# First feed-forward's begun blocks: fetches and stores in another order, TensorE's order written out, 1/rms applied by two engines

## The chip, the core and the metric

The kernel runs on one core of one Trainium2 chip. A core has TensorE (PE in the profile, its weight loads PEld), VectorE (DVE), ScalarE (ACT), GpSimd (POOL) and SyncE (SP, which here only issues transfers). The engines run side by side, each one in the order in which its instructions stand, and wait for each other through semaphores. SBUF is the working memory, PSUM (8 banks of 128x512 float32) takes TensorE's products. The metric is the time of one execution on the device, in microseconds (us).

## What is computed

An encoder layer on two sequences of 512 tokens of width 1024 (`x_prompt`, `x_sample`), in float32. The case is about its first step, a SwiGLU feed-forward behind an RMS norm:

```python
def rms_norm(x, g):
    xf = x.astype(jnp.float32)
    y = xf * lax.rsqrt(jnp.mean(xf * xf, axis=-1, keepdims=True) + EPS)
    return (y * g.astype(jnp.float32)).astype(x.dtype)

def swiglu(x, w_gate, w_up, w_down):
    return (jax.nn.silu(x @ w_gate) * (x @ w_up)) @ w_down
...
    x = x + 0.5 * swiglu(rms_norm(x, ffn1_norm), ffn1_w_gate, ffn1_w_up, ffn1_w_down)
```

Attention, an mLSTM memory, a second feed-forward and a last norm follow; the change doesn't touch them.

## The kernel before

**Products.** The gate and up products of both sequences are made together, column block by column block (22 blocks j of 128 columns, `NF`). The contraction of 1024 and the two operands (gate, up; prompt, sample) are each halved, and the 2x2 products are made in seven instead of eight (a Strassen scheme): B11, B21, B22, T1 to T4 name the seven pairs of left and right sums. Each float32 value is split in a high part (ScalarE copies it, rounded) and a low part (VectorE subtracts the copy), and a half product (`product`, L285) is 12 matmuls of 128x512: 4 steps of the contraction by high x high, high x low, low x high.

**Begun blocks.** The gate product of the prompt needs only B11 and B21, so the kernel begins 12 blocks (`AHEAD[0]`) with these two half products while the operands of the others are still being prepared, stores what comes out in `kept` (DRAM), and takes it back when the block is completed. Of these twelve, blocks 0 to 5 (`RAW`) are multiplied before 1/rms of the prompt is known, with x times the gain (`split_x`), and scaled by 1/rms afterwards; blocks 6 to 11 use the normed x. The parts, with their lines:

- `left(j)` (L1261): the weight block is fetched (`fetch_next`, L1206, 512 KB, four buffers `wr`), its high half copied by ScalarE (L248), its low half subtracted by VectorE (L249), into one of four tiles `w8`. `raws` holds blocks whose fetch was issued earlier.
- `lower(j)` (L1268): the half product B11 into a PSUM bank. Blocks 0, 1, 2, 7, 8, 10 and 11 use the three banks `mm`, blocks 3, 6 and 9 the one bank `pso` (PO), 4 and 5 the two `pss`. `evac(j)` (L1276): ScalarE copies the bank out (v1), and from block 6 on SP stores it. `upper(j)` (L1282): B21 on top, in the same bank, behind `evac(j)`.
- `end(j)` (L1285): blocks below 6 are scaled by 1/rms, the bank (L1290) and v1 (L1291), by VectorE; ScalarE's Silu; stores of v1 and of the gate value (L1293, L1297). Blocks from 6 on need only Silu. Their v1 and gate values take turns in two rows (`rings.k`), so a copy waits for the store of the row's last user.
- `squares(s, b)` (L1246): ScalarE's sums of squares of 128 rows of sequence s; `root(s)` (L1250): 1/rms by eleven small VectorE instructions; `spread(s, r)` (L1253): four transposes by TensorE into a bank and one ScalarE copy give 1/rms along the free axis. `normed(ks)` (L1256): x of the prompt times gain and 1/rms. The sample's x is multiplied by its gain by ScalarE (L1368) and by 1/rms by GpSimd (L1391), eight tiles of 128x512.
- `hi_all`, `lo_all`, `both` (L1302 to L1311) split the right operands. Behind the begun blocks stand the sums of T1 (L1407) and T2 (L1413), and the first full block (`gu_left_b`, L263; `gu_rest`, L307), whose first product is T2 (in the trace, the first `pss` product behind 100 us).

**What sets the order.** A scheduler places instructions by priority and by its own estimate of time. `pin` (`tc.keep_in_program_order`) holds an instruction behind those of its own engine that were pinned before it. Before the change, ScalarE's, VectorE's and GpSimd's work in this stretch and the fetches are pinned; TensorE's half products and transposes and the stores to `kept` are not.

**Queues.** All these transfers are issued by SP, in order: one that waits for its data holds those behind it. [...]

Of the kernel before, what the change touches and what calls it, by code (L numbers as in the profile page):

```python
# [26 lines left out]
def encoder(ctx, tc, I, outs):  # L27
# [154 lines left out]
                                    op=ALU.add))  # L182
        return c

    def bcast_psum(r):

        pr = PT()
        for b in range(4):
            nc.tensor.transpose(pr[:, b * P:(b + 1) * P], r[:, b:b + 1].to_broadcast([P, P]), ident)
        return pr  # L190

    def fetch_w(view):
# [89 lines left out]
            left.update({T1: wd, T3: part(wc, 0), T4: part(wc, 1)})  # L282
        return more

    def product(p, w, xt, first):  # L285
        wh, wl = w
        for k in range(HK_):
            for i, (a, b) in enumerate(((wh, 0), (wh, 1), (wl, 0))):
                nc.tensor.matmul(p, a[:, k, :], xt[:, b, k, :], start=(first and k == 0 and i == 0),  # L289
                                 stop=(k == HK_ - 1 and i == 2), skip_group_check=True)  # L290

    def gu_first(W, xc, rows, between=None):

# [10 lines left out]
            nc.scalar.activation(g0, X, AF.Silu)  # L304
        return v1, g0

    def gu_rest(W, xc, got, ring, mid):  # L307

        Y, Z = PS(), PT()
        second = lambda: product(Y, W[T2_], xc[T2_], True)  # L310
# [67 lines left out]
    class Up:  # L378
# [33 lines left out]
        def rest(self, raw, at=None, hook=None, left=None):  # L412
            ring, ORDER = self.ring, self.order

            def resume(j, pin=lambda i: i):
                got = ring.v(), ring.h()
                for t, d in zip(got, self.kept.pop(j)):
                    pin(nc.sync.dma_start(t[:, 0], d))
                return got

            if left is None:
                left = {}
                gu_left_b(*raw, ring, left)()
            raw = self.fetch(ORDER[1])
            got = resume(ORDER[0], tc.keep_in_program_order)
            for i, j in enumerate(ORDER):
                W, more = left, None
                nxt = ORDER[i + 1] if i + 1 < NF else None
                if nxt is not None:
                    left = {} if nxt in self.kept else gu_left_a(raw[0])  # L430
                    more = gu_left_b(*raw, ring, left)
                    raw = self.fetch(ORDER[i + 2]) if i + 2 < NF else None
                then = []
                h = gu_rest(W, self.xc, got, ring, lambda: then.append(resume(nxt)) if nxt in self.kept else None)
# [764 lines left out]

    in_rows = A([P, 4, D], F32, "xrows")  # L1200

    def load_rows(s):
        for b in range(4):
            pin(nc.sync.dma_start(in_rows[:, b, :], xins[s][b * P:(b + 1) * P, :]))

    def fetch_next(j):  # L1206
# [14 lines left out]
    load_x(0, 6, 8)  # L1221
    load_half(1, 1)
    raws = {2: fetch_next(2)}
    load_rows(0)
    raws[3] = fetch_next(3)

    rings = up.ring
    held_rows = [t[:, i] for t in rings.x.rows[:3] for i in range(2)]
# [22 lines left out]
        return rstd_cols(row_sq[s], 4, D, pin)  # L1251

    def spread(s, r):  # L1253
        pin(nc.scalar.activation(R[s], bcast_psum(r), AF.Copy))

    def normed(ks):  # L1256
        for k in ks:
# [10 lines left out]
    def lower(j):  # L1268
        if j < RAW:
            bank, row = (MM, MM, MM, PO, PS, PS)[j], held_rows[j]  # L1270
        else:
            bank, row = MM if j % 3 else PO, rings.k()
        begun[j] = bank(), row
        product(begun[j][0], W[j][B11], (xr[0] if j < RAW else xc[B11]), True)

    def evac(j):  # L1276
        X, v1 = begun[j]
        pin(nc.scalar.activation(v1, X, AF.Copy))
        if j >= RAW:
            nc.sync.dma_start(kept[j][0], v1)  # L1280

    def upper(j):  # L1282
        product(begun[j][0], W[j][B21], (xr[1] if j < RAW else xc[B21]), False)

    def end(j):  # L1285
        X, v1 = begun.pop(j)
        up.kept[j] = kept[j]
        if j < RAW:
            g0 = gate_rows()
            pin(V_.tensor_tensor(g0, X, R[0], op=ALU.mult))  # L1290
            pin(V_.tensor_tensor(v1, v1, R[0], op=ALU.mult))  # L1291
            pin(nc.scalar.activation(g0, g0, AF.Silu))
            nc.sync.dma_start(kept[j][0], v1)  # L1293
        else:
            g0 = rings.k()
            pin(nc.scalar.activation(g0, X, AF.Silu))
        nc.sync.dma_start(kept[j][1], g0)  # L1297

    def halves(s):
        return [x_t[s][:, i * HK_:(i + 1) * HK_, :] for i in range(2)]  # L1300
# [10 lines left out]
        lo_all(m, src)  # L1311

    (x0l, x0u), (x1l, x1u) = halves(0), halves(1)

    first_left(0, 0)
    for k in range(HK_):
# [13 lines left out]
    upper(1)  # L1330
    left(2)
    squares(0, 0)
    left(3)
    squares(0, 1)
    squares(0, 2)
    lower(2)
    lower(3)
    left(4)
    evac(2)
    squares(0, 3)  # L1340
    evac(3)
    r = root(0)
    raws[5] = fetch_next(5)
    raws[6] = fetch_next(6)
    for k in range(0, KD, 2):
        load_x(1, k, k + 2)
    raws[7] = fetch_next(7)
    load_rows(1)
    left(5)
    spread(0, r)  # L1350
    upper(2)
    upper(3)
    normed(range(4))
    end(0)
    hi_all(B11, x0l)
    lower(4)
    normed(range(4, 8))
    lower(5)
    evac(4)
    hi_all(B21, x0u)  # L1360
    upper(4)
    lo_all(B11, x0l)
    lo_all(B21, x0u)
    evac(5)
    upper(5)
    for k in range(KD):
        x = x_t[1][:, k, :]
        pin(nc.scalar.activation(x, x, AF.Copy, scale=g1[:, k:k + 1]))  # L1368
        if k == 1:
            left(6)  # L1370
        if k == 3:
            end(1)
            squares(1, 0)
        if k == 5:
            left(7)
            squares(1, 1)
    end(2)
    squares(1, 2)
    lower(6)
    squares(1, 3)  # L1380
    lower(7)
    evac(6)
    end(3)
    upper(6)
    r = root(1)
    spread(1, r)
    evac(7)
    upper(7)
    for k in range(KD):
        x = x_t[1][:, k, :]  # L1390
        pin(G_.tensor_tensor(x, x, R[1], op=ALU.mult))  # L1391
    end(4)
    end(6)
    left(8)
    end(5)
    end(7)
    left(9)
    lower(8)
    lower(9)
    evac(8)  # L1400
    left(10)
    upper(8)
    evac(9)
    upper(9)
    t2s, t4s = rings.h.rows[1:], rings.o.rows[1:]
    two = lambda t, i: t[:, 2 * i:2 * i + 2, :]
    pin(V_.tensor_tensor(x0l, x1l, x0l, op=ALU.subtract))  # L1407
    left(11)
    end(8)
    end(9)  # L1410
    raw0 = up.fetch(up.order[0])
    for i in range(2):
        pin(V_.tensor_tensor(t2s[i], two(x1u, i), two(x0l, i), op=ALU.subtract))  # L1413
    xc[T2_] = xc_tile()
    for i in range(2):
        k2 = slice(2 * i, 2 * i + 2)
        pin(nc.scalar.activation(xc[T2_][:, 0, k2, :], t2s[i], AF.Copy))
        pin(V_.tensor_tensor(xc[T2_][:, 1, k2, :], t2s[i], f(xc[T2_][:, 0, k2, :]), op=ALU.subtract))
    lower(10)
    lower(11)  # L1420
    evac(10)
    hi_all(T1, x0l)
    evac(11)
    upper(10)
    upper(11)
    W0 = {}
    more = gu_left_b(*raw0, rings, W0, pin)
# [6 lines left out]
    for i in range(2):  # L1434
        pin(V_.tensor_tensor(t4s[i], two(x0u, i), t2s[i], op=ALU.subtract))
    both(B22, x1u)
    xc[T4] = xc_tile()
    for i in range(2):
        put(xc[T4], slice(2 * i, 2 * i + 2), t4s[i])

    def sums_of(k, turned, gain):
        x0l, x0u, x1l, x1u = [up.ring.x() for _ in range(4)]
# [232 lines left out]
```

## Time and profile before

| | us |
|---|---|
| median of 3 runs (2121.76 to 2124.85) | 2123.9 |
| the profiled execution | 2121.88 |
| its span in the profile | 2120.1 |
| TensorE busy with matmuls in the span | 2069.4 (98%) |
| VectorE, ScalarE, GpSimd busy | 1559.2, 944.6, 110.0 |
| mean granted clock of TensorE in the span | 0.993 of full speed |

The profile is one execution. Its page gives each engine's busy time, the span in 40 slices, the transfers, the chain of waits that ended last, and the costliest groups of instructions. Other views list the instructions in order of time ("start us, us, engine line op out<-in xcount", with, in brackets, the idle time of that engine just before and what ended it), who waited for whom, and each engine's busy time in chosen windows, with the clock that TensorE was granted. A row with x12 merges twelve instructions of one kind that follow each other. In the chain that ended last TensorE has 86%, VectorE 6%, ScalarE 4%. In the first 200 us TensorE is busy 176.2 us.

### The profile page before, as it was taken

The numbers are of one execution on the slowest core, as the hardware profiler recorded it, in microseconds if no ns is written. First come the engines' busy times: TensorE is split into PE (matmuls) and PEld (weight loads), VectorE is DVE, ScalarE is ACT, GpSimd is POOL, SyncE is SP. The second block draws the span as 40 slices with busy tenths as digits, with TensorE's granted clock in tenths as the row PEclk, the third lists the DMA queues.
The fourth block names the chain that finished last, engine by engine and source line by source line (L and its number), as shares of the span: only waits on it lengthen the run. The fifth ranks groups of instructions, "written<-read, shape, count | busy, mean of one in ns | idle before, by whom it ended". The sixth has DMA issues, their size and how long they took to land.

```text
span 2120.1 us, 26131 instructions
## 1 busy us (share of the span) xinstructions
PE 2069.4 (98%) x9416; PEld 1687.4 (80%) x9416; DVE 1559.2 (74%) x2550; ACT 944.6 (45%) x1575; POOL 110.0 (5%) x113
## 2 busy tenths in 40 slices
PE   8799999999999999999999999999999999999997
PEld 6578888888888777878887777788788888888886
DVE  6498787886796796574649865754887877776687
ACT  6344443442225466463436555544534434343224
POOL 0200000001000110100101101010000000000002
PEclk9899999999999999999999999999999999999999
DMA  7445655699764221223342222344546444369753
GB/s 273 170 153 179 229 178 179 225 354 370 274 220 161 80 70 61 89 90 115 123 141 75 75 90 80 120 148 174 171 151 231 175 173 175 143 247 393 282 209 139
DMA packets 141777, 370.15 MB, mean 175 GB/s; under 512 B 13936, under 2 KB 13952, under 8 KB 140624
## 3 DMA queue, kind: packets, MB, share of 16 engines
q1 hardware_dynamic: 140656, 366.44, 48.7%
q0 software_dynamic: 560, 1.26, 0.3%
q8 instruction: 74, 1.21, 0.2%
q10 hardware_dynamic: 432, 0.79, 0.1%
q14 instruction: 55, 0.45, 0.1%
HBM read 263.02 MB, written 105.41 MB: 174 GB/s over the span
## 4 chain that ended last, share of the span: by engine, by line
PE 86%; DVE 6%; ACT 4%; DMA 2%; issue 1%; SPq 0%; POOL 0%; ACTq 0%; DVEq 0%; POOLq 0%
PE pss L289 17%; PE mm L698 14%; PE pst L289 11%; PE mm L289 8%; PE mm L542 8%; PE pst L542 4%; PE pss L542 4%; PE mm L682 4%; PE mm L1127 3%; PE pso L542 3%; PE pso L954 2%; PE pso L682 1%; DMA wr<-in_ffn_w_gate_dram 1%; PE pss L926 1%; PE pso L1083 1%
## 5 line engine op out<-in xcount | busy, mean ns | idle before, releaser
L289 PE MATMUL pss<-xc,w 128*128 128x512 f32 x1632 | 389.8, 389 | 0.2 <-DVE w L249 0.2
L289 PEld LDWEIGHTS pss<-xc,w 128*128 128x128 f32 x1632 | 306.2, 188 | 64.8 <-DVE w L249 0.6
L698 PE MATMUL mm<-xh,w 128*128 128x512 f32 x896 | 292.6, 396 | 0.9 <-DVE w L207 0.9
L248 ACT ACTIVATE w<-wr 128x1024 fp32r<-128x1024 f32 (+1 forms) x134 | 139.9, 1046 | 259.5 <-PE pst L289 132.6
L289 PE MATMUL mm<-xc,w 128*128 128x512 f32 x936 | 231.8, 397 | 13.9 <-ACT w L248 7.9
L249 DVE TENSOR_TENSOR w<-wr,w 128x1024 fp32r<-128x1024 f32 (+1 forms) x134 | 161.8, 1209 | 110.7 <-ACT w L248 110.5
L289 PEld LDWEIGHTS mm<-xc,w 128*128 128x128 f32 x936 | 176.9, 191 | 57.6 <-ACT w L248 8.8
L207 DVE TENSOR_TENSOR w<-wr,w 128x1024 fp32r<-128x1024 f32 (+1 forms) x112 | 135.3, 1208 | 116.5 <-ACT w L206 115.5
L698 PEld LDWEIGHTS mm<-xh,w 128*128 128x128 f32 x896 | 167.1, 188 | 33.5 <-DVE w L207 1.3
L542 PE MATMUL mm<-w,rt 128*128 128x512 f32 x792 | 185.3, 389 | 0.0
L698 PE MATMUL mm<-xl,w 128*128 128x512 f32 x448 | 176.9, 395 | 0.0
L542 PEld LDWEIGHTS mm<-w,rt 128*128 128x128 f32 x792 | 148.5, 188 | 30.7
L206 ACT ACTIVATE w<-wr 128x1024 fp32r<-128x1024 f32 (+1 forms) x112 | 114.6, 1030 | 109.8 <-PE pso L1127 35.0
L289 PE MATMUL pst<-xc,f 128*128 128x512 f32 x528 | 127.8, 389 | 0.5 <-ACT f L244 0.5
L289 PE MATMUL pst<-xc,w 128*128 128x512 f32 x528 | 127.5, 389 | 0.0
L289 PEld LDWEIGHTS pst<-xc,f 128*128 128x128 f32 x528 | 99.0, 188 | 21.6 <-ACT f L244 1.1
L289 PEld LDWEIGHTS pst<-xc,w 128*128 128x128 f32 x528 | 99.0, 188 | 20.9 <-DVE xc L1307 0.2
L602 ACT ACTIVATE w<-t 128x512 fp32r<-128x512 f32 x82 | 51.6, 632 | 122.4 <-PE pst L542 63.6
L602 ACT ACTIVATE w<-wr 128x512 fp32r<-128x512 f32 x72 | 44.5, 631 | 127.9 <-PE pso L542 68.0
L698 PEld LDWEIGHTS mm<-xl,w 128*128 128x128 f32 x448 | 84.3, 188 | 16.0
L542 PE MATMUL pss<-w,rt 128*128 128x512 f32 x396 | 94.4, 389 | 0.6 <-ACT w L602 0.6
L542 PE MATMUL pst<-w,rt 128*128 128x512 f32 x396 | 94.0, 389 | 0.0
(353 smaller groups left out, 3528.4 us busy)
## 6 DMA issues: line engine op xcount, KB each, us to landing
rt<-rbuf SPq DMA_DIRECT2D x154, 512.0 KB, 6.0
rbuf<-t SPq DMA_DIRECT2D x72, 512.0 KB, 3.5
wr<-in_ffn_w_gate_dram SPq DMA_DIRECT2D x60, 512.0 KB, 4.2
wr<-in_w_in_cols_dram SPq DMA_DIRECT2D x56, 512.0 KB, 3.5
wr<-in_ffn_w_up_dram SPq DMA_DIRECT2D x44, 512.0 KB, 3.6
rbuf<-f SPq DMA_DIRECT2D x30, 512.0 KB, 3.7
rbuf<-tab SPq DMA_DIRECT2D x30, 512.0 KB, 3.9
wr<-in_ffn_w_down_dram SPq DMA_DIRECT2D x48, 256.0 KB, 6.5
```

Source lines behind the costliest of these rows:

```text
L206: pin(nc.scalar.activation(hi, raw, AF.Copy))
L207: pin(lo_eng.tensor_tensor(lo, raw, f(hi), op=ALU.subtract))
L248: pin(nc.scalar.activation(t[:, 0], src, AF.Copy))
L249: pin(V_.tensor_tensor(t[:, 1], src, f(t[:, 0]), op=ALU.subtract))
L289: nc.tensor.matmul(p, a[:, k, :], xt[:, b, k, :], start=(first and k == 0 and i == 0), stop=(k == HK_ - 1 and i == 2), skip_group_check=True)
L542: nc.tensor.matmul(p, r[:, b, d * P:(d + 1) * P], u[:, a, :], start=(first and q == 0 and k == 0), stop=(q == len(us) - 1 and k == 2), ski ...
L602: nc.scalar.activation(hi, src, AF.Copy)
L682: nc.tensor.matmul(p[b][:, :N], a[:, k, bs], w_[:, kl, :], start=(k == 0 and i == 0), stop=(k == KD - 1 and i == 2))
L698: nc.tensor.matmul(p, a[:, k, :], b, start=(k == 0 and i == 0), stop=(k == n - 1 and i == 2))
L926: nc.tensor.matmul(p, qT[:, h, b * P:(b + 1) * P], kv[:, hk * 2 + j, :], start=(j == 0), stop=(j == 1))
L954: nc.tensor.matmul(po, Vst[:, kv_, hk, :], w, start=(kv_ == 0 and i == 0), stop=(kv_ == 3 and i == 1))
L1127: nc.tensor.matmul(p[b], a[:, k, bs], w_[:, k - k0, :], start=(k == 0 and i == 0), stop=(k == KD - 1 and i == 2))
```

## The change

It changes the order of the stretch before the first full block, and which engines apply the sample's 1/rms. It leaves out no work and adds none.

- Fetches: rows 2 and 3 of the prompt go behind weight block 3; blocks 4 and 5 ahead of the sample's x, 6 and 7 behind it; blocks 8 and 9 are fetched behind the sample's rows, ahead of all stores, 10 and 11 behind block 0's two stores. Before, the fetch of a block from 8 on was issued by its `left`.
- The stores to `kept` are pinned; so are TensorE's half products of the begun blocks, its transposes for 1/rms, and the first full block's T2 product.
- The gain of the sample (`gain1`) is applied two tiles at a time, between other work of ScalarE. `squares`, `left`, `end` and `evac` are in another order: lower(6) stands ahead of lower(7) and ahead of root(1) and end(3); root(1) behind left(8); left(9) behind the scalings by 1/rms; evac(10) behind the first full block's `gu_left_b`.
- VectorE multiplies tiles 0 to 3 of the sample by 1/rms, GpSimd 4 to 7.

The diff, cut where it only passes `pin` along:

```diff
-    load_rows(0)
+    load_rows(0, (0, 1))
     raws[3] = fetch_next(3)
+    load_rows(0, (2, 3))
...
-        product(begun[j][0], W[j][B11], (xr[0] if j < RAW else xc[B11]), True)
+        product(begun[j][0], W[j][B11], (xr[0] if j < RAW else xc[B11]), True, pin)
...
-            nc.sync.dma_start(kept[j][0], v1)
+            pin(nc.sync.dma_start(kept[j][0], v1))
...
+    def gain1(ks):
+        for k in ks:
+            x = x_t[1][:, k, :]
+            pin(nc.scalar.activation(x, x, AF.Copy, scale=g1[:, k:k + 1]))
+
+    def fetch_more(*js):
+        for j in js:
+            raws[j] = fetch_next(j)
+
+    def sum2(src, a, b):
+        for i in range(2):
+            pin(V_.tensor_tensor(src[i], a(i), b(i), op=ALU.subtract))
+
+    def both2(m, src):
+        xc[m] = xc_tile()
+        for i in range(2):
+            t = xc[m][:, :, 2 * i:2 * i + 2, :]
+            pin(nc.scalar.activation(t[:, 0], src[i], AF.Copy))
+            pin(V_.tensor_tensor(t[:, 1], src[i], f(t[:, 0]), op=ALU.subtract))
...
     evac(2)
+    fetch_more(4, 5)
     for k in range(0, KD, 2):
         load_x(1, k, k + 2)
+    fetch_more(6, 7)
+    load_rows(1, range(4))
+    left(4)
+    r = root(0)
+    upper(2, (0, 1))
+    evac(3)
+    spread(0, r)
+    upper(2, (2, 3))
+    upper(3)
     left(5)
+    fetch_more(8, 9)
+    gain1((0, 1))
     normed(range(4))
+    lower(4)
+    lower(5)
     end(0)
     hi_all(B11, x0l)
+    gain1((2, 3))
+    evac(4)
     normed(range(4, 8))
     hi_all(B21, x0u)
     upper(4)
     lo_all(B11, x0l)
+    gain1((4, 5))
     evac(5)
     upper(5)
+    lo_all(B21, x0u)
+    left(6)
+    left(7)
+    fetch_more(10, 11)
+    squares(1, 0)
+    end(1)
+    gain1((6, 7))
+    squares(1, 1)
+    squares(1, 2)
     end(2)
     lower(6)
     squares(1, 3)
     lower(7)
+    left(8)
     evac(6)
+    r = root(1)
     end(3)
     upper(6)
+    evac(7)
     spread(1, r)
     upper(7)
     for k in range(KD):
         x = x_t[1][:, k, :]
-        pin(G_.tensor_tensor(x, x, R[1], op=ALU.mult))
+        pin((V_ if k < HK_ else G_).tensor_tensor(x, x, R[1], op=ALU.mult))
+    left(9)
+    end(6)
     end(4)
+    pin(V_.tensor_tensor(x0l, x1l, x0l, op=ALU.subtract))
+    lower(8)
+    end(7)
+    lower(9)
+    left(10)
+    evac(8)
     end(5)
     upper(8)
     evac(9)
     upper(9)
+    raw0 = up.fetch(up.order[0])
+    sum2(t2s, lambda i: two(x1u, i), lambda i: two(x0l, i))
     left(11)
     end(8)
+    both2(T2_, t2s)
     end(9)
     lower(10)
     lower(11)
+    W0 = {}
+    more = gu_left_b(*raw0, rings, W0, pin)
     evac(10)
     hi_all(T1, x0l)
+    upper(10)
     evac(11)
     upper(11)
     lo_all(T1, x0l)
     more()
     end(10)
     end(11)
```

Of the long part only the new order is shown; the lines that it takes out are those of the old order above (L1332 to L1439).

More of the change, by code (lines that the diff above doesn't have):

```diff
@@ L283, in gu_left_b, with product @@
         return more
-    def product(p, w, xt, first):
+    def product(p, w, xt, first, pin=lambda i: i, ks=range(HK_)):
         wh, wl = w
-        for k in range(HK_):
+        for k in ks:
             for i, (a, b) in enumerate(((wh, 0), (wh, 1), (wl, 0))):
-                nc.tensor.matmul(p, a[:, k, :], xt[:, b, k, :], start=(first and k == 0 and i == 0),
-                                 stop=(k == HK_ - 1 and i == 2), skip_group_check=True)
+                pin(nc.tensor.matmul(p, a[:, k, :], xt[:, b, k, :], start=(first and k == 0 and i == 0),
+                                     stop=(k == HK_ - 1 and i == 2), skip_group_check=True))
     def gu_first(W, xc, rows, between=None):
@@ L433, in rest @@
                 then = []
-                h = gu_rest(W, self.xc, got, ring, lambda: then.append(resume(nxt)) if nxt in self.kept else None)
+                h = gu_rest(W, self.xc, got, ring, lambda: then.append(resume(nxt)) if nxt in self.kept else None,
+                            *([] if i else [tc.keep_in_program_order]))
                 got = then[0] if then else None
@@ L1200, in encoder, with load_rows @@
     in_rows = A([P, 4, D], F32, "xrows")
-    def load_rows(s):
-        for b in range(4):
+    def load_rows(s, bs):
+        for b in bs:
             pin(nc.sync.dma_start(in_rows[:, b, :], xins[s][b * P:(b + 1) * P, :]))
@@ L1279, in evac, with upper @@
         if j >= RAW:
-            nc.sync.dma_start(kept[j][0], v1)
-    def upper(j):
-        product(begun[j][0], W[j][B21], (xr[1] if j < RAW else xc[B21]), False)
+            pin(nc.sync.dma_start(kept[j][0], v1))
+    def upper(j, ks=range(HK_)):
+        product(begun[j][0], W[j][B21], (xr[1] if j < RAW else xc[B21]), False, pin, ks)
     def end(j):
@@ L1296, in end @@
             pin(nc.scalar.activation(g0, X, AF.Silu))
-        nc.sync.dma_start(kept[j][1], g0)
+        pin(nc.sync.dma_start(kept[j][1], g0))
     def halves(s):
@@ L1313, in encoder @@
     (x0l, x0u), (x1l, x1u) = halves(0), halves(1)
+    def gain1(ks):
+        for k in ks:
+            x = x_t[1][:, k, :]
[12 more added lines that the diff above has]
+            pin(V_.tensor_tensor(t[:, 1], src[i], f(t[:, 0]), op=ALU.subtract))
+    t2s, t4s = rings.h.rows[1:], rings.o.rows[1:]
+    two = lambda t, i: t[:, 2 * i:2 * i + 2, :]
     first_left(0, 0)
@@ L1332, in encoder @@
     squares(0, 0)
+    squares(0, 1)
     left(3)
-    squares(0, 1)
+    lower(2)
     squares(0, 2)
-    lower(2)
+    squares(0, 3)
     lower(3)
-    left(4)
     evac(2)
[L1340 to L1344, printed above, removed]
+    fetch_more(4, 5)
     for k in range(0, KD, 2):
         load_x(1, k, k + 2)
-    raws[7] = fetch_next(7)
-    load_rows(1)
+    fetch_more(6, 7)
[7 more added lines that the diff above has]
+    upper(3)
     left(5)
-    spread(0, r)
-    upper(2)
-    upper(3)
+    fetch_more(8, 9)
+    gain1((0, 1))
     normed(range(4))
+    lower(4)
+    lower(5)
     end(0)
     hi_all(B11, x0l)
-    lower(4)
+    gain1((2, 3))
+    evac(4)
     normed(range(4, 8))
-    lower(5)
-    evac(4)
     hi_all(B21, x0u)
@@ L1433, in encoder @@
     both(T3, x1l)
-    for i in range(2):
-        pin(V_.tensor_tensor(t4s[i], two(x0u, i), t2s[i], op=ALU.subtract))
+    sum2(t4s, lambda i: two(x0u, i), lambda i: t2s[i])
     both(B22, x1u)
-    xc[T4] = xc_tile()
-    for i in range(2):
-        put(xc[T4], slice(2 * i, 2 * i + 2), t4s[i])
+    both2(T4, t4s)
     def sums_of(k, turned, gain):
```

49 lines of the change are left out of this document (6 added, 43 removed).

## The prediction

> **What bounds the kernel now.** I read the page's slices of the span first (53 us each; TensorE is under 9 tenths busy only in the first two and the last), then who waited for whom in the first 200 us, then TensorE in order of time:
>
> ```profile
> PE   8799999999999999999999999999999999999997
> ...
> PE mm L289 <- ACT w L248: 7.9, 2, 4.8
> PE pso L289 <- ACT w L248: 5.6, 1, 5.6
> ...
> PE mm L289 <- DVE w L249: 1.4, 2, 1.1
> ```
>
> The two largest waits are for weight halves that ScalarE copies (`left`, L248). In order of time (start, duration, then the idle before it and what ended it):
>
> ```profile
> 32.78 11.04 PE L289 MATMUL pss<-xc,w 128*128 128x512 f32 x48
> 46.97 5.47 PE L289 MATMUL mm<-xc,w 128*128 128x512 f32 x11 [3.15 <-ACT w L248]
> ...
> 68.76 1.22 PE L289 MATMUL mm<-xc,w 128*128 128x512 f32 x2 [4.77 <-ACT w L248]
> ...
> 80.00 5.05 PE L289 MATMUL pso<-xc,w 128*128 128x512 f32 x12 [5.59 <-ACT w L248]
> ...
> 90.33 5.60 PE L289 MATMUL mm<-xc,w 128*128 128x512 f32 x24
> ...
> 102.49 0.73 PE L289 MATMUL pss<-xc,w 128*128 128x512 f32 x2
> ...
> 103.75 2.56 PE L289 MATMUL pss<-xc,w 128*128 128x512 f32 x10 [0.25 <-DVE w L249]
> ...
> 109.75 0.73 PE L289 MATMUL pst<-xc,f 128*128 128x512 f32 x2 [0.49 <-ACT f L244]
> ...
> 111.62 1.19 PE L289 MATMUL mm<-xc,w 128*128 128x512 f32 x4 [1.14 <-DVE w L249]
> ```
>
> 24 matmuls in 5.6 us are 0.227 us each: a half product (`lower` or `upper`, 12 matmuls) is 2.72 us. From the end of upper(5) (the first row's end less what its last matmul overlaps, 43.7) to the first T2 product of the full blocks (102.49) lie 58.8 us for 12 half products (32.6 us) and four transposes (0.4): 25.8 us are lost. Behind 102.49 another 1.9 us (0.25 + 0.49 + 1.14), then nothing. Part of the 25.8 is the clock, which falls to half when TensorE has stood still (columns: window; its length and the busy us of PE, PEld, DVE, ACT, POOL; granted clock):
>
> ```profile
> 43.60:47.00 3.40, 0.25 (x2) 0.03 (x1) 0.10 (x2) 3.40 (x7) 0.00 (x0) 0.91 0.42 157
> 47.00:53.20 6.20, 6.16 (x14) 4.38 (x15) 4.74 (x12) 4.78 (x9) 0.00 (x0) 0.50 0.33 127
> ...
> 68.80:73.70 4.90, 4.61 (x10) 3.21 (x11) 3.11 (x3) 1.12 (x2) 4.83 (x6) 0.50 0.16 54
> ...
> 80.00:84.00 4.00, 3.96 (x9) 2.69 (x10) 1.20 (x1) 0.43 (x1) 0.00 (x0) 0.51 0.54 194
> ```
>
> Why the weights come late is on SP's queue: a fetch stands behind stores of `kept`, and ScalarE waits for it.
>
> ```profile
> 61.92 1.97 SPq L1297 DMA_DIRECT2D kept<-f  x1
> 63.94 0.43 SPq L1208 DMA_DIRECT2D wr<-in_ffn_w_gate_dram  x1
> 67.65 1.06 ACT L248 ACTIVATE w<-wr 128x1024 fp32r<-128x1024 f32 x1 [5.76 <-DMA wr<-in_ffn_w_gate_dram]
> ...
> 73.27 0.43 SPq L1208 DMA_DIRECT2D wr<-in_ffn_w_gate_dram  x1
> ...
> 78.89 1.06 ACT L248 ACTIVATE w<-wr 128x1024 fp32r<-128x1024 f32 x1 [6.92 <-DMA wr<-in_ffn_w_gate_dram]
> ```
>
> **The change part by part.** No matmul, copy or transfer is added; four of the eight scalings of x1 go from GpSimd to VectorE, the rest is order.
>
> *Weights ahead of stores.* Fetches 8 and 9 stand ahead of every store, 10 and 11 behind block 0's two. Their buffers are free once left(4) and left(5) are split (24 and 30 us in the sums below), so they needn't wait until 63.94 and 73.27: the waits of 5.76 and 6.92 go, with TensorE's 4.77 and 5.59 and half of the 4.9 and 4.0 us at half clock. That would be worth some 15 us if nothing else were late. What is late next is the sum.
>
> *TensorE's order set.* lower(6) now comes first, ahead of lower(7); its bank is PO, which end(3) must have read. In the changed order VectorE does end(3) behind left(8) and root(1), and root(1) needs all four `squares(1, ..)`. TensorE goes in order, so all its later work, ScalarE's evac(6) and the stores behind that stand in this queue. When end(3) comes is a chain through ScalarE and VectorE, priced by these rows:
>
> ```profile
> 10.00:20.00 10.00, 10.00 (x46) 8.24 (x45) 5.30 (x8) 6.23 (x11) 0.00 (x0) 1.00 1.03 412
> ...
> 19.80 1.06 ACT L248 ACTIVATE w<-wr 128x1024 fp32r<-128x1024 f32 x1 [3.59 <-DMA wr<-in_ffn_w_gate_dram]
> 20.77 1.04 ACT L1248 ACTIVATE xrows<-xrows 128x1024 f32<-128x1024 f32 x1
> ...
> 23.92 1.23 DVE L249 TENSOR_TENSOR w<-wr,w 128x1024 fp32r<-128x1024 f32 x1 [1.80 <-ACT w L248]
> 25.44 0.17 DVE L173 TENSOR_SCALAR rs<-rsq 128x4 f32<-128x4 f32 x1 [0.29 <-ACT xrows L1248]
> ...
> 27.43 0.16 DVE L168 SCALAR_TENSOR_TENSOR rs<-rs,rs 128x4 f32<-128x4 f32 x1
> ...
> 28.40 0.60 ACT L1254 ACTIVATE t<-pst 128x512 f32<-128x512 f32 x1 [1.56 <-PE pst L189]
> 29.03 2.74 DVE L1259 SCALAR_TENSOR_TENSOR xt<-xt,g,t 128x512 f32<-128x512 f32 x4 [0.27 <-ACT t L1254]
> 31.69 0.69 DVE L1290 TENSOR_TENSOR tab<-mm,t 128x512 f32<-128x512 f32 x1
> ...
> 32.95 1.90 ACT L1304 ACTIVATE xc<-xt 128x2048 fp32r<-128x2048 f32 x1
> 35.54 2.29 DVE L1307 TENSOR_TENSOR xc<-xt,xc 128x2048 fp32r<-128x2048 f32 x1
> 38.91 1.33 ACT L1368 ACTIVATE xt<-xt,g 128x512 f32<-128x512 f32 x2
> ```
>
> (Instructions that follow each other start some 0.1 us before the one ahead ends.) Block 3's weights pass two transfers of 512 KB, 1.27 us each at 412 GB/s: left(3) at 17.3 instead of 19.80. The last squares end at 20.9, evac(2) waits for lower(2) until 21.2 and ends at 21.8, left(4) ends at 22.8, its low half at 24.0, root(0) (11 instructions, 2.15 us) at 26.1, transposes 26.8, spread(0) 27.4; before, 29.0. Then left(5), 28.3 and 29.5; four `normed` 32.2; end(0) 32.9; its Silu 33.4; hi_all(B11) 35.2; two of gain1 36.4; evac(4) 36.9; hi_all(B21) 38.8. VectorE: lo_all(B21) 41.1; low halves of left(6) and left(7) 43.9; end(1) 44.5. ScalarE: Silu 45.0; two of gain1 46.3; two squares with their sums 48.4; Silu 48.9; last square 49.9; left(8) 51.0. VectorE: its low half 52.2; root(1) 54.3; end(3) 54.9. TensorE, held a little by evac(4) and evac(5), ends upper(5) at 43.3 and stands for 11.6 us, where the first wait now was 3.15.
>
> It then runs at half clock. The rows bound that by 4.0 and 6.2 us; I take 5.0. lower(6) takes 5.3 instead of 2.7: 60.2; lower(7) and upper(6) 65.7; four transposes 66.3; spread(1) 66.9.
>
> *1/rms in halves.* GpSimd's eight scalings become four, and VectorE's four start with them. They hinder each other:
>
> ```profile
> 60.48 10.88 POOL L1391 TENSOR_TENSOR xt<-xt,tab 128x512 f32<-128x512 f32 x8 [59.19 <-ACT tab L1254]
> ...
> 69.09 2.27 POOL L1391 TENSOR_TENSOR xt<-xt,tab 128x512 f32<-128x512 f32 x1
> ...
> 68.74 1.48 DVE L249 TENSOR_TENSOR w<-wr,w 128x1024 fp32r<-128x1024 f32 x1 [13.56 <-ACT w L248]
> ...
> 2066.12 6.56 POOL L1543 TENSOR_TENSOR xs<-xs,tab 128x512 f32<-128x512 f32 x4 [142.71 <-ACT f L1161]
> ...
> 2069.76 3.47 DVE L603 TENSOR_TENSOR w<-wr,w 128x512 fp32r<-128x512 f32 x2
> ```
>
> Two VectorE operations of this size that read SBUF twice took 3.47 us beside GpSimd's four. Four scalings: 2.4 us if each takes 0.6 (the 0.69 at 31.69 less the overlap), 6.9 by this row, which is nearest; left(9)'s low half 1.5 by the row at 68.74: 75.3, and from 70.4 if they didn't hinder. The Trainium skill says the same more strictly ("SBUF — State Buffer", Who interferes with whom): a VectorE instruction with two SBUF inputs and a GpSimd one that reads SBUF take turns at a lock held for the whole instruction. By turns it would be an estimated 8.7 us instead of 8.4, and the time 0.3 later; the 2.27 us of GpSimd's last scaling agree.
>
> *What then ends last* is VectorE, each step behind the one before: end(4) 76.5; T1's sum 78.7; left(10) 79.8; end(5) 81.0; T2's sums 83.3; left(11) 84.4. Now a fetch decides: the second full block's up weights use the buffer that left(11) frees. Issue to copy was 3.7 us before (63.94 to 67.65): 88.2. VectorE sums them between the first block's own sums: four operations of 0.6, 90.6; then ScalarE's copy of the first block's gate half, 91.7, and, queued behind that copy, evac(10), 92.3, for which upper(10) waits. TensorE's own work (transposes and seven half products from 65.7, with some 2 us of waits for left(9) and evac(8)) would be done by 87 or 88, so it doesn't set the end, not even if it loses another 2 us to the clock. Two half products: T2 at 97.7 instead of 102.5.
>
> The 1.9 us behind T2 go: its weights' low half ends at 93.0, 4.7 ahead of TensorE, where before it came after T2's start. Gain: 102.5 + 1.9 - 97.7 = 6.7 us.
>
> *At nothing:* gain1's spreading (ScalarE's work, counted in the chain), the stores' order on SP (evac(9) waits for the store of evac(8)'s row; TensorE's 4 us ahead of upper(10) cover a late one, and what goes beyond them counts in full).
>
> **The rivals.**
> (1) VectorE isn't held by GpSimd: left(9) at 70.4, all behind it 4.9 earlier, T2 at 92.8, gain 11.6. For it: TensorE could follow (its own work ends at 85). Against it: the 3.47 us.
> (2) The change removes the waits for weights and loses as much in waits for VectorE: fetch 5.6 us long as that issued at 73.27 (copy at 78.89), half clock 6.2 us, the 1.9 us stay: 1.9 + 0.6 + 1.9 later, gain 2.3. For it: every step of the last chain is in series. Against it: nothing else is on the queue at that fetch.
> (3) Slower: fetch 8 isn't early. left(8), root(1) and end(3) follow it, and TensorE with them. It decides if left(8) starts later than 49.9 + 6.7 = 56.6. If it came at 67.65 as now, the time would be 17.8 - 6.7 = 11 us longer. Against it: fetch 8 is the 15th transfer of 512 KB behind block 3's: 17.3 + 15 x 1.27 = 36.4, 13 us ahead of 49.9.
>
> **How the numbers follow.** The profiled execution took 2121.88 us (span 2120.1); the median of the three runs is 2123.9, 2.0 above. The four together have a mean of 2123.1, less 6.7 is 2116.4. Chances: forecast 0.69, (1) 0.14 at 2111.5, (2) 0.12 at 2120.8, (3) 0.05 at 2134. The forecast's own range is 2112 to 2121: half clock 0.5 less or 0.6 more, the fetch up to 1.9 more, the 1.9 us kept; with (1) it is 2110 to 2121. Between runs 0.2%, 4.2 us, can be told from no change. The forecast lies beyond that in 0.85 of its cases: faster 0.69 x 0.85 + 0.14 = 0.73; same 0.10 + 0.12 = 0.22; slower 0.05.
>
> **What would show it.** Right: lower(6) (pso, 128x512) with some 11 us idle before it, ended by VectorE's L1292; half clock for 4 to 6 us behind it; no ScalarE copy of weights 8 and 9 that waits for a DMA; GpSimd's four scalings in over 6 us and VectorE's four in 6 to 7; a wait of 2 to 5 us ahead of upper(10), ended by ScalarE's evac; T2 at 96 to 99 us; then no wait to 120 us. Wrong: end(3) well off 54.9; VectorE's four scalings in 2.4 us; a wait for left(8)'s fetch; or new waits behind 120 us, which the sum takes as unchanged.

## The result, and the profile after

| | us | runs |
|---|---|---|
| before, median (lowest to highest) | 2123.08 (2119.19 to 2125.74) | 11 |
| after, median (lowest to highest of ten) | 2118.03 (2115.42 to 2120.42) | 11 |
| after over before | 0.9975, 95% interval 0.9966 to 0.9985 | |

The change makes the kernel faster by 0.25%, 5.3 us (0.0025 x 2123); forecast were 6.7. One run of after, the profiled one, took 7607.19 us at a mean granted clock of 0.42, for no known reason, and is left out; so the changed kernel was run once more as it is, and what is shown of "after" is the profile of that run:

> The changed kernel once more, for a profile at full clock. Theory (the forecast's two chains): lower(6) starts at 54.9 behind VectorE's end(3), after 11.6 us without a matmul; half clock for about 5 us; VectorE's four scalings with 1/rms and left(9)'s low half take 8.4 us behind spread(1); upper(10) waits for evac(10) until 92.3; T2 starts at 97.7; no wait behind it. Rival (GpSimd doesn't hold VectorE): the same up to spread(1), then left(9) done 3.5 us behind it and T2 at 92.8. The measured medians (2123.08 and 2118.03) allow for a gain of 4 to 6 us, which is nearer to the first.

Measured: 2118.51 us, before 2124.31 beside it, ratio 0.9974 (0.9964 to 0.9984); the profiled execution took 2118.51, its span is 2116.7 against 2120.1 before. TensorE of after in order of time (start, duration, then the idle before it and what ended it):

```profile
22.96 2.88 PE L289 MATMUL pso<-xc,w 128*128 128x512 f32 x12
...
42.62 3.02 PE L289 MATMUL pss<-xc,w 128*128 128x512 f32 x12 [0.49 <-ACT t L1280]
57.06 4.46 PE L289 MATMUL pso<-xc,w 128*128 128x512 f32 x12 [11.42 <-DVE t L1292]
61.36 2.89 PE L289 MATMUL mm<-xc,w 128*128 128x512 f32 x12
...
76.12 3.67 PE L289 MATMUL pso<-xc,w 128*128 128x512 f32 x10 [2.79 <-DVE w L249]
...
86.07 5.60 PE L289 MATMUL mm<-xc,w 128*128 128x512 f32 x24
94.22 7.35 PE L289 MATMUL mm<-xc,w 128*128 128x512 f32 x24 [2.56 <-ACT f L1280]
101.41 2.88 PE L289 MATMUL pss<-xc,w 128*128 128x512 f32 x12
104.13 2.88 PE L289 MATMUL pst<-xc,f 128*128 128x512 f32 x12
```

The two waits for weights, 4.77 and 5.59 us, are gone. In their place stands one of 11.42 us: lower(6) waits for end(3) (VectorE's L1292). Two shorter ones follow, for left(9)'s low half (2.79) and for evac(10) (2.56). T2 (the first `pss` row after 100) comes at 101.41, and nothing waits behind it, where before 1.9 us were lost. The clock, in windows of the same run (length, then the busy us of PE, PEld, DVE, ACT, POOL; granted clock):

```profile
57.00:61.40 4.40, 4.34 (x13) 3.48 (x14) 0.51 (x1) 0.00 (x0) 0.00 (x0) 0.63 0.01 5
...
94.20:97.20 3.00, 2.98 (x7) 2.41 (x8) 1.94 (x2) 3.00 (x4) 0.00 (x0) 0.53 0.60 171
97.20:101.40 4.20, 4.20 (x18) 3.37 (x17) 4.20 (x4) 2.27 (x3) 0.00 (x0) 0.93 0.57 202
```

The last chain runs through the other engines, again in order of time:

```profile
56.23 0.68 DVE L1292 TENSOR_TENSOR t<-pso,t 128x512 f32<-128x512 f32 x1
...
67.44 0.60 ACT L1256 ACTIVATE tab<-pst 128x512 f32<-128x512 f32 x1 [2.56 <-PE pst L189]
...
68.08 5.79 DVE L1417 TENSOR_TENSOR xt<-xt,tab 128x512 f32<-128x512 f32 x4 [10.56 <-ACT tab L1256]
73.79 2.28 DVE L249 TENSOR_TENSOR w<-wr,w 128x1024 fp32r<-128x1024 f32 x1
...
84.12 1.23 DVE L249 TENSOR_TENSOR w<-wr,w 128x1024 fp32r<-128x1024 f32 x1
...
85.37 0.33 SPq L199 DMA_DIRECT2D wr<-in_ffn_w_up_dram  x1
...
90.10 0.69 DVE L269 TENSOR_TENSOR tab<-wr 128x512 f32<-128x512 f32 x1 [0.86 <-DMA wr<-in_ffn_w_up_dram]
...
92.63 1.06 ACT L248 ACTIVATE w<-wr 128x1024 fp32r<-128x1024 f32 x1 [4.61 <-DVE wr L272]
93.59 0.58 ACT L1280 ACTIVATE f<-mm 128x512 f32<-128x512 f32 x1
```

In this order they are end(3), spread(1), VectorE's four scalings, left(9)'s low half, left(11)'s low half, the fetch that its end released, the first sum that used it, the gate half's copy, and evac(10).

### The profile page after: what moved, and what is told of

The parts are those of the page before. It is cut to its first block, busy times and chain, and to the rows that moved or that the text cites. A ratio compares the mean times of both kernels' runs of the same rounds, so it can differ in the third digit from the quotient of the medians.

```text
span 7605.4 us, 26137 instructions
## 1 busy us (share of the span) xinstructions
PE 7594.6 (100%) x9416; PEld 4357.4 (57%) x9416; DVE 1591.6 (21%) x2554; ACT 959.8 (13%) x1575; POOL 97.1 (1%) x109
## 4 chain that ended last, share of the span: by engine, by line
PE 100%; DVE 0%; ACT 0%; issue 0%; ACTq 0%; DVEq 0%
PE pss L289 20%; PE mm L699 19%; PE pst L289 13%; PE mm L289 12%; PE mm L543 7%; PE mm L683 4%; PE pss L543 4%; PE pst L543 4%; PE mm L1128 3%; PE pso L543 2%; PE pso L955 1%; PE pss L927 1%; PE pst L948 1%; PE pso L683 1%; PE pso L289 1%; PE pso L1084 1%
## 5 line engine op out<-in xcount | busy, mean ns | idle before, releaser
L289 PE MATMUL pss<-xc,w 128*128 128x512 f32 x1632 | 1555.4, 1227 | 0.0
L289 PEld LDWEIGHTS pss<-xc,w 128*128 128x128 f32 x1632 | 912.8, 559 | 609.1 <-issue 608.7
L289 PE MATMUL mm<-xc,w 128*128 128x512 f32 x936 | 907.7, 1250 | 0.0
L699 PE MATMUL mm<-xh,w 128*128 128x512 f32 x896 | 892.2, 1112 | 0.0
L289 PEld LDWEIGHTS mm<-xc,w 128*128 128x128 f32 x936 | 538.2, 576 | 344.5 <-issue 343.8
L543 PE MATMUL mm<-w,rt 128*128 128x512 f32 x792 | 570.0, 962 | 0.0
L289 PE MATMUL pst<-xc,f 128*128 128x512 f32 x528 | 501.0, 1214 | 0.0
L289 PE MATMUL pst<-xc,w 128*128 128x512 f32 x528 | 500.3, 1217 | 0.0
L699 PE MATMUL mm<-xl,w 128*128 128x512 f32 x448 | 494.0, 1103 | 0.0
L683 PE MATMUL mm<-w,xh 128*128 128x512 f32 (+1 forms) x288 | 239.3, 966 | 0.0
```

The lines of the kernel that those rows point to most:

```text
L289: pin(nc.tensor.matmul(p, a[:, k, :], xt[:, b, k, :], start=(first and k == 0 and i == 0), stop=(k == HK_ - 1 and i == 2), skip_group_chec ...
L543: nc.tensor.matmul(p, r[:, b, d * P:(d + 1) * P], u[:, a, :], start=(first and q == 0 and k == 0), stop=(q == len(us) - 1 and k == 2), ski ...
L683: nc.tensor.matmul(p[b][:, :N], a[:, k, bs], w_[:, kl, :], start=(k == 0 and i == 0), stop=(k == KD - 1 and i == 2))
L699: nc.tensor.matmul(p, a[:, k, :], b, start=(k == 0 and i == 0), stop=(k == n - 1 and i == 2))
```

## The experiments

In each, the ratio is to the kernel before, run beside it on the same chip; after itself has 0.9974 or 0.9975. e1 to e5 and e7 change one thing of after, e6 and e8 put together what paid, and e9 starts from the kernel before. Executions differ in their first 20 us (last section), so a time in the trace is compared with after's only beside the start of lower(3), 22.96 there.

**end(3) ahead of the weights and 1/rms.** Is the wait of 11.42 us what the whole change pays?

```diff
     end(2)
+    end(3)
     lower(6)
...
     r = root(1)
-    end(3)
```

> The changed kernel with end(3) ahead of lower(6), left(8) and root(1): VectorE frees the bank PO before it starts on the sample's 1/rms. Theory (lower(6) waits for end(3), and this wait is the start of the chain that sets the end): lower(6) at 46.9 instead of 54.9, spread(1) ends at about 58 instead of 66.9, all behind it 8 us earlier: 2110 us. Rival (the stretch behind spread(1) is bound by something that doesn't hang on lower(6), a fetch or a store): the wait at lower(6) shrinks and another takes its place; less than 3 us faster than the changed kernel.

Measured: 2108.19 us, ratio 0.9925 (0.9913 to 0.9938), 10 us below after. TensorE of this kernel:

```profile
21.99 2.88 PE L289 MATMUL pso<-xc,w 128*128 128x512 f32 x12
...
48.10 4.52 PE L289 MATMUL pso<-xc,w 128*128 128x512 f32 x12 [3.41 <-DVE t L1292]
...
92.58 2.88 PE L289 MATMUL pss<-xc,w 128*128 128x512 f32 x12
```

lower(6) waits 3.41 instead of 11.42 us, and T2 is 8.8 us earlier (0.97 of it from the earlier start). What the wait held was the end of the stage.

**All eight scalings on one engine.** Two kernels: VectorE alone, and GpSimd alone as before the change.

```diff
-        pin((V_ if k < HK_ else G_).tensor_tensor(x, x, R[1], op=ALU.mult))
+        pin(V_.tensor_tensor(x, x, R[1], op=ALU.mult))
```

> The changed kernel with all eight scalings of the sample by 1/rms on VectorE, none on GpSimd. Theory (the two engines hinder each other at operations that read SBUF twice): VectorE's eight take 4.8 us, left(9)'s low half is done 6 us behind spread(1) instead of 8.4, T2 2.4 us earlier: 2115.6 us. Rival (they don't hinder each other): eight take 4.8 us instead of 2.4, T2 2.4 us later: 2120.4 us.

Measured: 2114.25 us, ratio 0.9956 (0.9942 to 0.9969). VectorE of this kernel:

```profile
66.97 4.90 DVE L1417 TENSOR_TENSOR xt<-xt,tab 128x512 f32<-128x512 f32 x8 [10.85 <-ACT tab L1256]
71.79 1.22 DVE L249 TENSOR_TENSOR w<-wr,w 128x1024 fp32r<-128x1024 f32 x1
```

Alone it does eight in 4.90 us; with GpSimd's help it took 5.79 for four, and left(9)'s low half 2.28 instead of 1.22. Halving the work made VectorE's share longer than the whole. From the end of spread(1) to the end of left(9)'s low half it is 6.1 us instead of 8.0, close to the 2.4 us less that were expected. T2 comes at 96.42, 3.3 us earlier beside the start (lower(3) at 21.26), but 1.6 of that is the clock: the 24 matmuls ahead of it took 5.58 us to T2's start, at full speed behind an idle of 2.27 us, where after's took 7.19.

```diff
+        pin(G_.tensor_tensor(x, x, R[1], op=ALU.mult))
```

> All eight scalings of the sample by 1/rms on GpSimd, as before the change, the rest as changed. Theory (VectorE's own queue is the chain, and a VectorE operation that reads SBUF twice beside GpSimd costs about double): spread(1) ends at 68; GpSimd's eight end at 79 to 81; VectorE goes straight on with left(9)'s low half (to 70.5), end(4) (71.8), T1's sum (waits for GpSimd's fourth tile at about 73.6, about 76), left(10), end(5) (78.5), T2's sums (the second waits for the eighth tile at about 81, ends at 82.2), left(11) at 83.4 where the changed kernel has 85.35: 2 us sooner, time 2116.5. Rival (halving is worth what it looks like: the scalings end 4 us sooner with two engines): T2's sums come later than in the changed kernel, time 2121 or more.

Measured: 2117.89 us, ratio 0.9973 (0.9962 to 0.9984): neither the 2 us sooner of the theory nor the rival's loss, the same as after (T2 at 99.11 is 1.2 us sooner beside the start, lower(3) at 21.88). GpSimd and VectorE of this kernel:

```profile
67.39 14.91 POOL L1417 TENSOR_TENSOR xt<-xt,tab 128x512 f32<-128x512 f32 x8 [66.09 <-ACT tab L1256]
...
69.69 0.68 DVE L1292 TENSOR_TENSOR tab<-pss,t 128x512 f32<-128x512 f32 x1
70.29 1.18 DVE L1293 TENSOR_TENSOR t<-t,t 128x512 f32<-128x512 f32 x1
73.91 3.36 DVE L1421 TENSOR_TENSOR xt<-xt,xt 128x2048 f32<-128x2048 f32 x1 [2.44 <-POOL xt L1417]
77.20 2.29 DVE L249 TENSOR_TENSOR w<-wr,w 128x1024 fp32r<-128x1024 f32 x1
...
81.08 3.44 DVE L1328 TENSOR_TENSOR t<-xt,xt 128x1024 f32<-128x1024 f32 x2
```

I had priced T1's sum, left(10)'s low half and T2's sums at what they cost alone (2.29, 1.22 and 2.36 us, the last from VectorE's timeline of e2). Beside GpSimd they take 3.36, 2.29 and 3.44 (of T2's two sums only the first starts before GpSimd ends at 82.30), and GpSimd's eight take 14.91 instead of 10.88. The hindrance lasts as long as GpSimd works. It depends on where the inputs lie: end(4)'s scaling of the bank (L1292, PSUM and SBUF) keeps its 0.68 us, that of v1 (L1293, twice SBUF) takes 1.18.

**evac(10) and evac(11) ahead of the first full block's weights.**

```diff
     W0 = {}
-    more = gu_left_b(*raw0, rings, W0, pin)
     evac(10)
-    hi_all(T1, x0l)
     upper(10)
     evac(11)
+    more = gu_left_b(*raw0, rings, W0, pin)
+    hi_all(T1, x0l)
```

> The changed kernel with evac(10), upper(10) and evac(11) ahead of the first full block's left sums, so that ScalarE's evac(10) isn't queued behind the copy of that block's gate half. Theory (upper(10) waits only for what stands ahead of evac(10) on ScalarE; TensorE's own work is done at 87 or 88): T2 some 3.5 us earlier, of which up to 1.5 may come back as waits for VectorE behind T2: 2115 us. Rival (TensorE isn't ready before 92 anyway, for instance through evac(8) and evac(9)): no difference, 2118 us.

Measured: 2115.77 us, ratio 0.9963 (0.9950 to 0.9975). TensorE of this kernel:

```profile
21.44 2.88 PE L289 MATMUL pso<-xc,w 128*128 128x512 f32 x12
...
75.23 2.56 PE L289 MATMUL pso<-xc,w 128*128 128x512 f32 x10 [2.79 <-DVE w L249]
...
85.18 11.04 PE L289 MATMUL mm<-xc,w 128*128 128x512 f32 x48
96.06 2.88 PE L289 MATMUL pss<-xc,w 128*128 128x512 f32 x12
```

lower(10), lower(11) and both uppers run through as 48 matmuls; T2 is 5.35 us earlier, 1.5 of it from the start. It was the fetch behind left(11), through ScalarE's order, that upper(10) waited for. The time is 2.7 us below that of after beside it (2118.51), near the 2115 of the theory: behind T2 waits of 0.44 and 0.75 us come back.

**The fetch order undone, the rest as changed**, so that left(8) to left(11) issue their own:

```diff
-    fetch_more(8, 9)
...
-    fetch_more(10, 11)
```

> Only the fetch order of blocks 8 to 11 is undone: each is issued by its left, behind the stores that stand ahead of it, the rest as changed. Theory (a fetch takes 4 to 5 us from issue to the copy, and left(8), (10) and (11) lie on the chain): left(8) waits until about 56 instead of 51.9 (+4), left(10) about 4.5 more, left(11) partly in the same wait: T2 8 to 13 us later, time 2127 to 2132, slower than before. Rival (the waits for weights are cover for other waits in any case, since VectorE and TensorE are late): within 3 us of the changed kernel, 2118 to 2121.

Measured: 2125.02 us, ratio 1.0008 (0.9999 to 1.0016): 7 us above after, short of the theory's 2127 to 2132 and further from the rival's 2118 to 2121. ScalarE and TensorE of this kernel:

```profile
54.80 1.06 ACT L248 ACTIVATE w<-wr 128x1024 fp32r<-128x1024 f32 x1 [3.06 <-DMA wr<-in_ffn_w_gate_dram]
...
87.03 1.06 ACT L248 ACTIVATE w<-wr 128x1024 fp32r<-128x1024 f32 x1 [6.29 <-DMA wr<-in_ffn_w_gate_dram]
...
92.10 1.05 ACT L248 ACTIVATE w<-wr 128x1024 fp32r<-128x1024 f32 x1
...
103.44 5.74 PE L289 MATMUL mm<-xc,w 128*128 128x512 f32 x24 [1.16 <-ACT f L1280]
109.02 2.88 PE L289 MATMUL pss<-xc,w 128*128 128x512 f32 x12
```

left(8) and left(10) wait, 3.06 and 6.29 us (about 4 and 4.5 in the theory), left(9), at 72.13, 1.16 us; left(11) (92.10) waits for no transfer, and the last 24 matmuls ran at full speed. Without the fetches, the rest of the change shows no gain: the interval of its ratio reaches from 0.9999 to 1.0016.

**lower(7) ahead of lower(6) on TensorE** (their rows left as they were):

```diff
-    lower(6)
+    r6, r7 = rings.k(), rings.k()
+    lower(7, r7)
     squares(1, 3)
-    lower(7)
+    lower(6, r6)
```

> Only lower(7) goes ahead of lower(6) on TensorE (rows as they were), so that one half product is done while lower(6) waits for end(3). Theory: lower(7) runs at about 46 to 49; lower(6) still starts at 57.1, behind end(3), and at half clock (idle 8 instead of 11.4); upper(6) waits for evac(6) to about 62.2 and runs to 65, so transposes, spread(1) and all behind come 1.9 us sooner: time 2116.6. Rival (TensorE's work between end(3) and spread(1) is not on the chain): 2118.5, unchanged.

Measured: 2115.18 us, ratio 0.9961 (0.9949 to 0.9973). TensorE of this kernel:

```profile
22.15 2.88 PE L289 MATMUL pso<-xc,w 128*128 128x512 f32 x12
...
44.68 3.04 PE L289 MATMUL mm<-xc,w 128*128 128x512 f32 x12
56.16 5.44 PE L289 MATMUL pso<-xc,w 128*128 128x512 f32 x12 [8.45 <-DVE t L1292]
62.29 3.05 PE L289 MATMUL pso<-xc,w 128*128 128x512 f32 x12 [0.69 <-ACT f L1280]
...
99.60 2.88 PE L289 MATMUL pss<-xc,w 128*128 128x512 f32 x12
```

lower(7) goes into the wait as expected. In the trace T2 comes 1.8 us earlier, 0.8 of it from the start, less than the 1.9 expected, because all twelve matmuls of lower(6) were slow this time (5.44 us against 4.46). The time is near the theory's 2116.6, and its interval just leaves out after's ratio; but of the some 3 us the trace shows 1.0 at T2. The rest is behind T2: this execution's time less T2's start is 2015.6 us, after's 2017.1, and no row here explains that.

**The fetch order alone, in the kernel before.** One part of the change without the others:

```diff
     left(5)
+    raws[8] = fetch_next(8)
+    raws[9] = fetch_next(9)
...
             left(7)
+            raws[10] = fetch_next(10)
+            raws[11] = fetch_next(11)
```

> The kernel before with one part of the change alone: fetches 8 and 9 ahead of all stores (behind the sample's rows), 10 and 11 behind left(7); TensorE not pinned, scalings all on GpSimd, the rest of the order as before. Theory (late weights were the wait, and the changed order put end(3) and a stall of 11 us on the chain in their place): left(8) is split at 62 instead of 67.65, left(9) at 67 instead of 78.89; GpSimd's scalings end at 72, T1's sum at 74.5, T2's sums at 78, the full block's weights at 83, TensorE's own work at 87; T2 at 87 to 90 instead of 102.5, new waits behind it of 2 to 4 us: time 2108 to 2114, faster than the whole change. Rival (the weights ahead are worth something only with the rest of the order): 2118 or more.

Measured: 2107.45 us, ratio 0.9921 (0.9908 to 0.9934), 16 us below the kernel before (2123.49 beside it), three times what the whole change gains. TensorE, GpSimd and ScalarE of this kernel in order of time:

```profile
22.20 2.88 PE L289 MATMUL pso<-xc,w 128*128 128x512 f32 x12
...
48.80 5.47 PE L289 MATMUL mm<-xc,w 128*128 128x512 f32 x11 [3.15 <-ACT w L248]
54.06 3.56 PE L289 MATMUL pso<-xc,w 128*128 128x512 f32 x12
...
62.47 15.49 POOL L1395 TENSOR_TENSOR xt<-xt,tab 128x512 f32<-128x512 f32 x8 [61.18 <-ACT tab L1254]
...
63.76 1.07 ACT L248 ACTIVATE w<-wr 128x1024 fp32r<-128x1024 f32 x1
...
67.94 1.05 ACT L248 ACTIVATE w<-wr 128x1024 fp32r<-128x1024 f32 x1
...
89.17 3.22 PE L289 MATMUL pss<-xc,w 128*128 128x512 f32 x12
```

left(8) and left(9) are split at 63.76 and 67.94 with no wait for a transfer (67.65 and 78.89 before), and T2 comes at 89.17, 13.3 us earlier than before although the start was 1.2 us later. In the old order little else was late behind the weights: lower(7) runs at 48.80, and lower(6) follows it at 54.06 with no wait, since end(3) stands ahead of root(1) there.

**What paid, together.** end(3) early, lower(7) first, root(1) ahead of left(8), all scalings on VectorE, evac(10) and evac(11) early:

```diff
     end(2)
-    lower(6)
+    end(3)
+    r6, r7 = rings.k(), rings.k()
+    lower(7, r7)
     squares(1, 3)
-    lower(7)
+    lower(6, r6)
+    r = root(1)
     left(8)
     evac(6)
-    r = root(1)
-    end(3)
...
+        pin(V_.tensor_tensor(x, x, R[1], op=ALU.mult))
```

> All that paid, together: end(3) directly behind end(2); lower(7) ahead of lower(6); root(1) ahead of left(8); all eight scalings on VectorE; evac(10) and evac(11) ahead of the first full block's gu_left_b. Theory (the chain end(3), lower(6), spread(1), scalings, T1 and T2 sums, left(11), evac(10)): no TensorE wait of 11 us and no half clock behind it, spread(1) ends at about 55 instead of 68, T2 at 83 to 86 instead of 101.4; some 1 to 2 us of new waits behind T2, time 2101 to 2104. Rival (something outside this chain, such as the stores or the fetches of the first full block, decides by then): not under 2107.

Measured: 2105.46 us, ratio 0.9914 (0.9901 to 0.9927), above the 2101 to 2104 expected, below the rival's 2107. Singly, end(3) early gained 10 us on after, the scalings on VectorE 4, lower(7) first and evac(10) first some 3 each; together they gain 13, so these gains overlap. root(1) ahead of left(8) had no run of its own. TensorE of this kernel:

```profile
24.66 2.88 PE L289 MATMUL pso<-xc,w 128*128 128x512 f32 x12
...
55.74 4.60 PE L289 MATMUL pso<-xc,w 128*128 128x512 f32 x12 [2.06 <-ACT f L1280]
...
88.22 2.88 PE L289 MATMUL pss<-xc,w 128*128 128x512 f32 x12
```

I had put evac(6) behind the last squares and left(8) on ScalarE: upper(6) waits 2.06 us and then runs slowly. The next kernel mends that:

```diff
     end(3)
     r6, r7 = rings.k(), rings.k()
     lower(7, r7)
+    lower(6, r6)
+    evac(7)
+    upper(7)
     squares(1, 3)
-    lower(6, r6)
     r = root(1)
-    left(8)
     evac(6)
     upper(6)
-    evac(7)
+    left(8)
     spread(1, r)
-    upper(7)
```

> As e6_better, with ScalarE's and TensorE's order mended where that run's trace shows its one long wait left (upper(6) 2.06 us behind evac(6), which stood behind the squares and left(8), and half clock behind it, 4.6 us for 12 matmuls): lower(7), lower(6), upper(7), upper(6) on TensorE; evac(7) ahead of the last squares, evac(6) behind root(1)'s squares, left(8) behind evac(6). Theory (the same chain): TensorE doesn't stand for over 1 us between lower(7) and spread(1); 2 us of wait and some 1.9 us of half clock go, spread(1) and T2 come 3 to 4 us sooner than in e6_better; some of it is lost behind T2, where VectorE is busy without a gap: time 2102 to 2104. Rival (VectorE's work behind T2 is by now the bound): 2105 to 2106, as e6_better.

Measured: 2104.30 us, ratio 0.9909 (0.9895 to 0.9923), the fastest here. Its five runs (2102.10 to 2105.70) lie below the five of e9_fetches_alone beside it (2105.80 to 2108.27), by 3 us at the median; from e6_better, run at another time, it isn't told apart. TensorE of this kernel:

```profile
22.42 2.88 PE L289 MATMUL pso<-xc,w 128*128 128x512 f32 x12
...
64.48 4.14 PE L289 MATMUL pso<-xc,w 128*128 128x512 f32 x10 [3.56 <-DVE w L249]
...
85.42 2.88 PE L289 MATMUL pss<-xc,w 128*128 128x512 f32 x12
```

T2 is 2.8 us earlier than in e6_better, but 2.2 of that is the start, so 0.6 of the 3 to 4 us expected came. The wait has moved once more: lower(9) waits 3.56 us for left(9)'s low half, which stands behind the eight scalings on VectorE. The two kernels lie 17 and 19 us below before; where the next microseconds lie (left(9) ahead of the scalings, which takes evac(8) along) wasn't tried. Nor were, each alone, the new order of the first fetches, the gain of the sample two tiles at a time, and the pinned stores.

## Why the prediction came out as it did

The mechanism was right: the waits for weights give way to a chain through end(3) and VectorE, and most of the gain is lost there. The forecast of 2116.4 lies 1.6 below the measured median, and that it lies so near is in part luck: terms that were too small and terms that were too large make up for each other. Against the execution of after, step by step:

| step ends or starts | forecast | after | later by |
|---|---|---|---|
| upper(5) ends | 43.3 | 45.5 | 2.2 |
| lower(6) starts | 54.9 | 57.06 | 2.2 |
| lower(7) starts | 60.2 | 61.36 | 1.2 |
| spread(1) ends | 66.9 | 68.04 | 1.1 |
| left(9)'s low half ends | 75.3 | 76.07 | 0.8 |
| left(11)'s low half ends | 84.4 | 85.35 | 0.95 |
| evac(10) ends | 92.3 | 94.17 | 1.9 |
| T2 starts | 97.7 | 101.41 | 3.7 |

- *end(3)* was forecast at 54.9 and came at 56.91, with TensorE idle for 11.42 us (forecast 11.6). The 2 us are there already at lower(3), in the first matmuls, which the sum took from the profile of before; e2, with the same order up to there, reached lower(3) at 21.26, so they belong to the execution, not to the change.
- *Half clock at lower(6):* 5.3 us forecast for its twelve matmuls, 4.3 measured from its start to lower(7)'s, 1.0 less. That is outside the bounds: half clock for 4.0 us or more would have made it 4.7 or more. The 1.6 us above 2.72 are, at half speed, half clock for an estimated 3.2 us. With the same idle the step took 4.6, 4.6 and 4.9 us in e2, e3 and e4, so the term was too large there as well.
- *1/rms in halves:* VectorE's four scalings 6.9 forecast, 5.79 measured; left(9)'s low half 1.5 forecast, 2.28 measured; together 8.0 instead of 8.4, or of the 8.7 that were estimated by turns; GpSimd's four took 6.86. Rival (1), no hindrance, would have had 2.4 for the four; e2 shows 4.90 for eight when GpSimd is still. That rival falls.
- *The fetch behind left(11):* 3.7 us from issue to use forecast, 4.73 measured (85.37 to 90.10). This term was 1.0 too small, and not only here: in e1, e2, e4, e6, e7 and e8 it was 4.24 to 4.81. What made it longer isn't settled. The transfer engines were busy 89% of that time (85.40 to 90.10), against 60% in the stretch of before that the 3.7 came from (63.90 to 67.70); that this is the cause wasn't tested.
- *TensorE's cover ahead of upper(10):* its own work was forecast done by 87 or 88 and ended at 91.7; 1.1 of the delay was there at spread(1), and the matmuls behind the wait of 2.79 us ran slowly. The cover was 2.56 instead of over 4 us. It still didn't set the end.
- *The term that was missing:* the 24 matmuls behind that wait took 7.19 us from their start to T2's, instead of two half products at 2.72, 5.44: 1.75 us. For the matmuls that set the end, half clock was priced behind the 11 us stall alone. In e4, where that wait is gone, so is the term. It is a matter of chance as well: e1 and e7 lost 1.7 and 1.5 us there, e2 0.1, behind waits of 2.62, 2.66 and 2.27 us.
- *The stores' order*, put at nothing: ScalarE waited for stores, 0.67 us at evac(9) and 0.95 at end(9), and TensorE stood 0.16 us for evac(9). The cover held.
- *Behind T2* nothing waits, as forecast; so rival (2), which kept the 1.9 us, falls, though its longer fetch came halfway. Rival (3) falls too: ScalarE waits for no transfer at left(8) or left(9), and e5 shows what it would look like.

Start 2.2, half clock -1.0, scalings -0.4, steps of VectorE 0.2, fetch 1.0 and the missing 1.75 make 3.75, against the 3.7 at T2. So without the start the terms that were too small make 2.95 us, those that were too large take back 1.4, and T2 is 1.5 us later than forecast, about what the medians say: 5.3 us gained of 6.7. Of the signs, the order of events came as stated; three sizes did not: half clock for 4 to 6 us (3.2), VectorE's four scalings in 6 to 7 us (5.79), and T2 at 96 to 99 us (101.41, or 99.2 less the start's 2.2).

What the prediction did not see is how much of the loss was the new order's own doing. It said that the weights would be worth some 15 us "if nothing else were late", and e9 shows 16 with the old order around them, in which little else was. The whole change gains 5, 11 us less, and moving one statement in it, end(3), gains 10 (e1). The best order tried (e8) is 3 us below e9: that is what all the rest, mended, adds to the fetch order.

## What to carry to other kernels

Price each part of a composite change alone against the old order, not only the sum: here one part is worth three times the whole. When an engine's order is written out by hand, look for the instruction that only frees a buffer for another engine (end(3) empties a PSUM bank) and put it ahead of work that nobody waits for yet. Two engines that hinder each other at the same memory aren't two halves: four scalings beside four cost VectorE 5.79 us, eight alone 4.90.

## What the runs showed of the hardware

*Half clock after short waits.* Behind idles of 2.56 and 2.79 us (after) and 2.06 us (e6_better) the matmuls ran slowly; the windows behind them show granted clocks of 0.53, 0.67 and 0.63. Behind an idle of 2.79 us at the same place in e4 ten matmuls took 2.56 us, full speed, and e2's 24 behind 2.27 us ran at full speed too (5.74 us). So the length of the wait alone doesn't decide. The Trainium skill ("TensorE: Matmul & The Clock Gate", Part 1: The HAM clock gate) states a free-running window of 3.4 us, with half clock after at least one idle window: a window that doesn't start with the wait would fit that the same wait falls either way, but the length doesn't agree, as waits of 2.06 to 2.79 us were enough here.

*The start differs between executions.* lower(3) started at 21.02 and 22.20 us in the profiles of before and e9, and between 21.26 (e2) and 24.66 (e6_better) in the nine of after and its variants, which are the same up to there: up to 3.4 us, as much as some of the gains that are studied here. Behind T2 they differ too: the time of these nine executions less T2's start is 2015.6 to 2018.5 us.

*GpSimd's scalings* (eight tiles of 128x512) took 10.88 us beside a VectorE that was idle for all but the last 2.6 us of them, and 14.91 and 15.49 beside a busy one. Beside them, in e3, VectorE's T1 sum and left(10)'s low half took about 1.1 us longer (2.29 to 3.36, 1.22 to 2.29), the scaling of v1 0.5 (0.68 to 1.18); the scaling of the bank, with one input in PSUM, took no longer. The Trainium skill ("SBUF — State Buffer", Who interferes with whom) has the loser of the shared port wait for the whole instruction. The 1.1 us are near one of GpSimd's, which took 1.23 us each ahead of VectorE's next (seven from 60.48 to 69.09); the 0.5 are part of one.
